# The up-projection's operands prepared one by one, and eight parked tiles set between full ones

## The chip, the cores and the metric

The kernel runs on one core of a Trainium2 chip. The metric is the device time of one execution in microseconds; lower is better. TensorE multiplies, VectorE and ScalarE do elementwise work, GpSimd helps with some of it, and SyncE's queue issues nearly all DMA transfers.

## The reference

Two layers of a diffusion backbone over 1024 latent tokens and 256 context tokens, width 1024. Each layer has a token-mixing part (attention, a linear recurrence, a Fourier mix) and a gated ConvFFN. The change concerns the FFN of the latent tokens:

```python
def conv_ffn(h, w_up, conv_w, conv_b, w_down):
    u = h @ w_up
    up = jnp.pad(u, ((0, 0), (1, 1), (0, 0)))
    u = up[:, :-2] * conv_w[0] + up[:, 1:-1] * conv_w[1] + up[:, 2:] * conv_w[2] + conv_b
    a, g = jnp.split(u, 2, axis=-1)
    return (a * jax.nn.silu(g)) @ w_down
...
        ffn = conv_ffn(x1 * (1 + sc2) + sh2, w_up[l], conv_w[l], conv_b[l], w_down[l])
```

`h` is 1024 x 1024, `w_up` 1024 x 5632 (2816 value columns, then 2816 gate columns), all in float32.

## The kernel before

**Products.** Each float32 operand is split into a rounded hi part (a cast on ScalarE) and a lo part (source minus hi, a subtraction). A product is the sum of three matmuls, lo x hi, hi x lo and hi x hi (`mm3`, lines 159 to 161).

**Tiles.** The up-projection has 22 tiles `j`. A tile is 128 value columns and the 128 gate columns that belong to them, over all 1024 tokens. It is computed by a 2 x 2 scheme with seven products instead of eight. The weights are the quarters A11, A12 (value columns, first and second half of the contraction) and A21, A22 (gate columns); S1 to S4 are sums of them. The stream `h` is cut into B11 and B21 (later half of the tokens, first and second half of the contraction) and B12, B22 (earlier half); T1 to T4 are differences of them. Each of these operands has four quarters of 128 contraction rows by 512 tokens, so a product is 4 x 3 = 12 matmuls of 512 columns and a tile 84. `ORDER` lists the seven pairs of a tile.

**Accumulation.** In `up_all` some products add onto the bank of an earlier one: S2 onto A11, S3 onto S2, S4 onto S1. Between them the bank is read: the result goes to U, two buffers of 1026 columns (value and gate), each with one column of padding at either end. A product with `onto` can only start when that read has been done. Seven PSUM banks serve the loop. When a tile is complete, `gate` runs the width-3 convolution (`conv`: one pass on ScalarE, two on VectorE), a SiLU on the gate part, and the product, and stores it to the scratch tensor `act`.

**Parked tiles.** For the first `EARLY` = 6 tiles the products A11 B11 and A12 B21 are computed ahead by `up_early`, because B11 and B21 are ready first: two tiles during the output projection's end, the others while `combined_halves` prepares T1 to T4 and B22. The first product and the sum of both are stored to the scratch tensor `parked`. In the loop these tiles come first, j = 0 to 5. Each has five products; the first parked product is loaded into the later half of `U[0]`, read by the additions behind S2 and S3, and then overwritten there by a load of the second:

```python
                if j < EARLY:
                    nc.sync.dma_start(out=U[0][:, late], in_=parked[j, 0])
```

**Preparation.** `combined_halves` goes quarter by quarter: it loads the four raw quarters of one k, scales and shifts them, forms T1 to T4 of that k and splits all five. GpSimd makes the lo parts of T1 and T4, VectorE the others.

**Weights.** `up_weights` loads 512 KB for the value part and for the gate part of each tile, forms S1 to S4 on VectorE and splits 512 columns at a time; `up_all` keeps five split weights ahead of the product in hand.

**Order.** The kernel is written as one listing per layer; a framework puts the instructions in an order on each engine by priorities and its own estimate of when operands are ready, so an engine's order can differ from the listing. During layer 0's loop the conditioning projection for layer 1 (`bg`, tiles `pada` and `araw`) takes single steps between products.

## Time and profile before

| | us |
|---|---|
| median of 3 runs | 3336.25 |
| lowest and highest of them | 3333.35, 3342.41 |
| the profiled execution, its own time | 3349.57 |
| its span | 3347.8 |
| TensorE busy in it | 3098.0 (93%) |
| VectorE busy | 2363.9 (71%) |
| ScalarE busy | 1585.6 (47%) |
| GpSimd busy | 772.6 (23%) |

A busy time is the sum of an engine's instructions in the profiled execution, as a share of the span from the first instruction to the last. Matmuls overlap in it, so TensorE's busy share doesn't say how many matmuls it could have taken in addition; counting matmuls in a window does. A wait is the idle time of an engine ahead of an instruction, put down to the work whose end released it. Tile names in a row are the program's: `pu` is a product's bank, `whi` and `wlo` the parts of a weight, `T2h` and `T2l` those of T2, `hraw` a raw quarter, `hcomb` a difference, `cv` a convolution's result, `up` the scratch tensor of parked products.

### The profile page before, as it was taken

The numbers are of one execution on the slowest core, as the hardware profiler recorded it, in microseconds if no ns is written. First come the engines' busy times: TensorE is split into PE (matmuls) and PEld (weight loads), VectorE is DVE, ScalarE is ACT, GpSimd is POOL, SyncE is SP. The second block draws the span as 40 slices with busy tenths as digits, with TensorE's granted clock in tenths as the row PEclk, the third lists the DMA queues.
The fourth block names the chain that finished last, engine by engine and source line by source line (L and its number), as shares of the span: only waits on it lengthen the run. The fifth ranks groups of instructions, "written<-read, shape, count | busy, mean of one in ns | idle before, by whom it ended". The sixth has DMA issues, their size and how long they took to land.

```text
span 3347.8 us, 55191 instructions
## 1 busy us (share of the span) xinstructions
PE 3098.0 (93%) x20897; PEld 2526.6 (75%) x20897; DVE 2363.9 (71%) x4377; ACT 1585.6 (47%) x3169; POOL 772.6 (23%) x820
## 2 busy tenths in 40 slices
PE   6999998999979999999999999998978789999996
PEld 4878977787756777677797788876767677887785
DVE  4623567887687877668876754668777778887678
ACT  3324556674444544434454435655652434554332
POOL 3522114432210000021245351115425300000222
PEclk9999999999989999999999999998889899999998
DMA  7652232107655444597775432122028632223973
GB/s 216 201 159 80 59 98 58 39 15 237 212 186 158 129 130 131 162 252 197 235 211 173 133 106 71 47 85 73 21 82 228 207 110 85 85 76 116 277 185 126
DMA packets 450255, 456.51 MB, mean 136 GB/s; under 512 B 31859, under 2 KB 343620, under 8 KB 449990
## 3 DMA queue, kind: packets, MB, share of 16 engines
q1 hardware_dynamic: 420006, 404.53, 38.4%
q0 software_dynamic: 29984, 48.46, 7.7%
q8 instruction: 164, 2.69, 0.3%
q14 instruction: 101, 0.83, 0.1%
HBM read 358.36 MB, written 94.55 MB: 135 GB/s over the span
## 4 chain that ended last, share of the span: by engine, by line
PE 47%; DVE 11%; DMA 5%; POOL 3%; issue 2%; ACT 2%; SPq 1%; POOLq 0%; DVEq 0%; ACTq 0%
PE pu L159 9%; PE pu L160 8%; PE pu L161 8%; PE pd L159 3%; PE pd L160 3%; PE pd L161 3%; PE ps_t L603 2%; PE ps_s L567 1%; PE ps_o L613 1%; DMA araw<-act 1%; DVE cv L1120 1%; DVE wlo L1387 1%; PE ps_s L568 1%; PE pws L159 1%; PE ps_o L615 1%
## 5 line engine op out<-in xcount | busy, mean ns | idle before, releaser
L570 DVE TENSOR_REDUCE mx<-ps_s 128x1 f32<-128x512 f32 (+1 forms) x400 | 222.4, 588 | 109.7 <-PE ps_s L568 108.6
L1345 POOL DMA_DIRECT2D X<-in_w_down_dram x48 | 55.4, 1154 | 1028.9 <-DMA X<-in_w_down_dram 945.1
L609 DVE TENSOR_TENSOR pl<-ps_t,ph 128x512 fp32r<-128x512 f32 x328 | 223.0, 686 | 88.1 <-ACT ph L608 86.1
L603 PE MATMUL ps_t<-ident,p 128*128 128x128 f32 x1312 | 265.5, 286 | 14.2 <-DVE pl L609 8.7
L608 ACT CAST ph<-ps_t 128x512 fp32r<-128x512 f32 x328 | 191.0, 589 | 162.8 <-PE ps_o L615 81.7
L577 ACT ACTIVATE p<-ps_s,mx 128x512 f32<-128x512 f32 (+1 forms) x400 | 243.2, 617 | 52.2 <-DVE mx L573 42.4
L160 PE MATMUL pd<-wlo,whi 128*128 128x512 f32 x616 | 248.4, 403 | 14.0 <-DVE wlo L1387 12.3
L159 PE MATMUL pd<-whi,wlo 128*128 128x512 f32 x616 | 242.8, 401 | 16.9 <-DVE wlo L1387 12.7
L1120 DVE SCALAR_TENSOR_TENSOR cv<-U,cw,cv 128x512 f32<-128x512 f32 x352 | 247.1, 748 | 12.9 <-ACT cv L1117 12.8
L161 PE MATMUL pd<-whi 128*128 128x512 f32 x616 | 247.7, 402 | 0.0
L159 PE MATMUL pxs<-whi,hlo 128*128 128x256 f32 x752 | 221.5, 295 | 5.8 <-DVE hraw L1566 4.3
L145 POOL TENSOR_TENSOR wlo<-raw,whi 128x1024 fp32r<-128x1024 f32 x63 | 152.5, 2423 | 281.0 <-ACT whi L144 281.0
L160 PE MATMUL pxs<-wlo,hhi 128*128 128x256 f32 x752 | 216.5, 288 | 0.6 <-DVE wlo L145 0.4
L161 PE MATMUL pxs<-whi,hhi 128*128 128x256 f32 x752 | 216.2, 288 | 0.0
L613 PE MATMUL ps_o<-pl,V 128*128 128x256 f32 x656 | 202.8, 326 | 6.6 <-DVE pl L609 4.0
L603 PEld LDWEIGHTS ps_t<-ident,p 128*128 128x128 f32 x1312 | 166.2, 144 | 38.2 <-DVE pl L609 14.7
L1117 ACT ACTIVATE cv<-U,cb,cw 128x512 f32<-128x512 f32 x176 | 138.1, 815 | 111.4 <-DVE U L1248 99.3
L615 PE MATMUL ps_o<-ph,V 128*128 128x256 f32 x656 | 184.7, 299 | 0.0
L1232 ACT CAST whi<-S 128x512 fp32r<-128x512 f32 x176 | 106.4, 620 | 149.2 <-PE pu L161 113.3
L144 ACT CAST whi<-raw 128x1024 fp32r<-128x1024 f32 x130 | 136.0, 1049 | 84.3 <-DMA raw<-in_w_up_dram 30.7
L567 PE MATMUL ps_s<-KT,qt 128*128 128x512 f32 (+1 forms) x400 | 150.8, 408 | 6.4 <-ACT p L577 3.0
L159 PEld LDWEIGHTS pxs<-whi,hlo 128*128 128x128 f32 x752 | 143.5, 191 | 15.3 <-issue 7.4
(401 smaller groups left out, 9160.4 us busy)
## 6 DMA issues: line engine op xcount, KB each, us to landing
raw<-in_w_up_dram SPq DMA_DIRECT2D x144, 512.0 KB
raw<-in_w_ada_dram SPq DMA_DIRECT2D x96, 512.0 KB
raw<-in_w_down_dram SPq DMA_DIRECT2D x52, 512.0 KB
act<-cv SPq DMA_DIRECT2D x88, 256.0 KB
X<-in_w_down_dram POOLq DMA_DIRECT2D x40, 512.0 KB, 9.6
raw<-in_w_in_dram SPq DMA_DIRECT2D x36, 512.0 KB
y<-r SPq DMA_DIRECT2D x28, 512.0 KB
araw<-act SPq DMA_DIRECT2D x26, 512.0 KB
```

The lines of the kernel that those rows point to most:

```text
L159: nc.tensor.matmul(o, lhsT=al, rhs=bh, start=start, stop=False, skip_group_check=onto)
L160: nc.tensor.matmul(o, lhsT=ah, rhs=bl, start=False, stop=False, skip_group_check=onto)
L161: nc.tensor.matmul(o, lhsT=ah, rhs=bh, start=False, stop=stop, skip_group_check=onto)
L567: nc.tensor.matmul(t[:, 0:n], lhsT=qt[:, h % (2 * QT_PAIRS), :], rhs=KT[:, 2 * kv + 1, s0:s0 + n], start=True, stop=False)
L570: nc.vector.tensor_reduce(out=mx[:, j:j + 1], in_=t[:, 0:n], axis=AX.X, op=ALU.max)
L577: nc.scalar.activation(out=t, in_=sc[j][:, 0:n], func=AF.Exp, bias=mx[:, 3:4], accum_out=su[:, h, j:j + 1])
L603: nc.tensor.transpose(t[:, ss, h, :], in_=ps2[h][2 * s2 + ss], identity=ident)
L608: nc.scalar.copy(ph, tv)
L609: nc.vector.tensor_tensor(out=pl, in0=tv, in1=f32(ph), op=ALU.subtract)
L613: nc.tensor.matmul(o, lhsT=V[:, s, kv, 1:3, :].rearrange("p a c -> p (a c)"), rhs=pl[:, ss, :], start=(s == 0), stop=False)
L615: nc.tensor.matmul(o, lhsT=V[:, s, kv, 0:2, :].rearrange("p a c -> p (a c)"), rhs=ph[:, ss, :], start=False, stop=(s == nk - 1))
L1120: nc.vector.scalar_tensor_tensor(out=o, in0=u[:, tap:tap + n], scalar=convw[l][tap][:, c:c + 1], in1=o, op0=ALU.mult, op1=ALU.add)
```

## The change

- `EARLY` goes from 6 to 8. The loop's order is `TURNS`: tile 8, then 9, 0, 10, 1, ... 16, 7, then 17 to 21, so that each parked tile stands between full ones.
- The first parked product is loaded into a ring `old` of two tiles of its own, and the additions read it there.
- `combined_halves` loads all sixteen raw quarters first, most into memory of operands that are written later, and finishes one operand after the other: T2, T1, T3, B22, T4. All lo parts are made on VectorE. Between the parked tiles two steps of it run instead of three.
- Six weights of the loop are split before the preparation ends (`ready_w`).
- `ORDER` has S4 B22 ahead of A22 T4.
- A weight split covers 1024 columns (A11 with A12, S2 with S1, S3 with S4), A22 512. The convolution covers 1024 columns, the value part first, and a tile is stored to `act` in one transfer.

```diff
--- before.py
+++ after.py
@@ -37,7 +37,7 @@
 GRID_W = 64
 ROPE_THETA = 10000.0
 NLEV = 7
-EARLY = 6
+EARLY = 8
 HELD = (2, 3)
 W_DVE = (0, 1)
 N_W = 2
@@ -1145,11 +1145,14 @@
     NK = NJ // 2
 
     def h_pair(hp, nm):
-        return tuple(hp.tile([P, 4, HALF], F32R, name=nm + x) for x in "hl")
+        return tuple([t[:, k, :] for k in range(4)] for t in (hp.tile([P, 4, HALF], F32R, name=nm + x) for x in "hl"))
 
     def load_quarter(rp, yT, t0, k, cols, tag, bufs, eng=None):
         r = rp.tile([P, HALF], F32, tag=tag, bufs=bufs, name="hraw")
         nc.sync.dma_start(out=r, in_=yT[k * P:(k + 1) * P, CTX + t0:CTX + t0 + HALF])
+        return modulated(r, k, cols, eng)
+
+    def modulated(r, k, cols, eng=None):
         a, b = (c[:, k:k + 1] for c in cols)
         if eng is nc.scalar:
             nc.scalar.activation(out=r, in_=r, func=AF.Identity, scale=a, bias=b)
@@ -1158,7 +1161,7 @@
         return r
 
     def split_to(pair, k, src, eng):
-        hi, lo = (t[:, k, :] for t in pair)
+        hi, lo = (t[k] for t in pair)
         nc.scalar.copy(hi, src)
         eng.tensor_tensor(out=lo, in0=src, in1=f32(hi), op=ALU.subtract)
 
@@ -1168,24 +1171,60 @@
             split_to(h["B11" if k < 4 else "B21"], k % 4, r, nc.gpsimd)
             yield
 
-    def combined_halves(h, rp, yT, cols):
+    def combined_halves(h, hp, rp, yT, cols):
+
+        def place(nm, k, dt=F32):
+            return (rp if nm[0:3] == "raw" else hp).tile([P, HALF], dt, tag=f"{nm}{k}", bufs=1, name=nm)
+
+        def fetch(nm, r, k, eng=None):
+            kk, t0 = k + 4 * (nm[1] == "2"), HALF if nm[2] == "1" else 0
+            nc.sync.dma_start(out=r, in_=yT[kk * P:(kk + 1) * P, CTX + t0:CTX + t0 + HALF])
+            return modulated(r, kk, cols, eng)
+
+        def sub(o, x, y):
+            nc.vector.tensor_tensor(out=o, in0=x, in1=y, op=ALU.subtract)
+            return o
+
+        def split_into(nm, k, src):
+            hi, lo = (place(nm + x, k, F32R) for x in "hl")
+            nc.scalar.copy(hi, src)
+            nc.vector.tensor_tensor(out=lo, in0=src, in1=f32(hi), op=ALU.subtract)
+            for t, x in zip(h[nm], (hi, lo)):
+                t.append(x)
+
+        for nm in ("T2", "T1", "T3", "T4", "B22"):
+            h[nm] = ([], [])
+        b11, b21, b12, b22, t1, t2 = ([] for _ in range(6))
         for k in range(4):
-            b11, b21, b12, b22 = (load_quarter(rp, yT, t0, kk, cols, f"raw{t0}{kk // 4}", 1 if t0 else 2, e)
-                                  for t0, kk, e in ((HALF, k, nc.scalar), (HALF, k + 4, nc.scalar), (0, k, None), (0, k + 4, None)))
+            b11.append(fetch("B11", place("T3h", k), k, nc.scalar))
+            b21.append(fetch("B21", place("B22l", k), k, nc.scalar))
             yield
-            t1, t2, t3, t4 = (rp.tile([P, HALF], F32, tag=f"t{x}", bufs=1, name="hcomb") for x in range(4))
-            for o, x, y in ((t1, b12, b11), (t2, b22, t1), (t3, b22, b12), (t4, t2, b21)):
-                nc.vector.tensor_tensor(out=o, in0=x, in1=y, op=ALU.subtract)
+        for k in range(4):
+            b12.append(fetch("B12", place("B22h", k), k, nc.scalar))
+            b22.append(fetch("B22", place("raw2", k), k))
+            t1.append(sub(place("T3l", k), b12[k], b11[k]))
+            t2.append(sub(place("raw1", k), b22[k], t1[k]))
+            split_into("T2", k, t2[k])
             yield
-            for nm, src, eng in (("T2", t2, nc.vector), ("T1", t1, nc.gpsimd), ("T3", t3, nc.vector), ("T4", t4, nc.gpsimd),
-                                 ("B22", b22, nc.vector)):
-                split_to(h[nm], k, src, eng)
+        for k in range(4):
+            split_into("T1", k, t1[k])
+            yield
+        for k in range(4):
+            split_into("T3", k, sub(place("T4h", k), b22[k], b12[k]))
+            yield
+
+        t4 = [sub(t2[k], t2[k], b21[k]) for k in range(4)]
+        for k in range(4):
+            split_into("B22", k, b22[k])
+            yield
+        for k in range(4):
+            split_into("T4", k, t4[k])
             yield
 
     def up_product(w, b, bank, onto=None):
         acc = psu([P, HALF], "pu", bank) if onto is None else onto
         for k in range(4):
-            mm3(acc, tuple(t[:, k, :] for t in w), tuple(t[:, k, :] for t in b), k == 0 and onto is None, k == 3,
+            mm3(acc, tuple(t[:, k, :] for t in w), tuple(t[k] for t in b), k == 0 and onto is None, k == 3,
                 onto is not None)
         return acc
 
@@ -1199,7 +1238,10 @@
         for x, t in enumerate((p1, c11)):
             nc.sync.dma_start(out=parked[j, x], in_=t)
 
-    ORDER = (("A11", "B11"), ("A12", "B21"), ("S2", "T2"), ("S1", "T1"), ("S3", "T3"), ("A22", "T4"), ("S4", "B22"))
+    ORDER = (("A11", "B11"), ("A12", "B21"), ("S2", "T2"), ("S1", "T1"), ("S3", "T3"), ("S4", "B22"), ("A22", "T4"))
+
+
+    TURNS = [EARLY] + [x for j in range(EARLY) for x in (EARLY + 1 + j, j)] + list(range(2 * EARLY + 1, NJ))
 
     def up_weights(l, fp):
         made = {}
@@ -1216,57 +1258,75 @@
             if (j, nm) not in made:
                 for o, x, y, op in (("S1", "A21", "A22", ALU.add), ("S2", "S1", "A11", ALU.subtract),
                                     ("S3", "A11", "A21", ALU.subtract), ("S4", "A12", "S2", ALU.subtract)):
-                    t = fp.tile([P, 4, P], F32, tag=o, bufs=1, name=o)
+
+                    pair = "S21" if o in ("S1", "S2") else "S34"
+                    if (j, pair) not in made:
+                        made[j, pair] = fp.tile([P, KD, P], F32, tag=pair, bufs=1, name="S")
+                    h = 4 * pair[1:].index(o[1])
+                    t = made[j, pair][:, h:h + 4, :]
                     nc.vector.tensor_tensor(out=t, in0=operand(j, x), in1=operand(j, y), op=op)
                     made[j, o] = t
             return made[j, nm]
 
         def splits(todo):
-            for n, (j, nm) in enumerate(todo):
-                if n % 2 == 0:
-                    own = n // 2 % 5 > 2
-                    pair = [(fp if own else wp).tile([P, 1024], F32R, tag=t + "x" * own, bufs=2 if own else 3, name=t)
-                            for t in ("whi", "wlo")]
-                hi, lo = (t[:, n % 2 * 512:n % 2 * 512 + 512].rearrange("p (a b) -> p a b", a=4) for t in pair)
-                src = operand(j, nm)
+            wide = 0
+            while todo:
+                j, nm = todo.pop(0)
+                if nm == "A22":
+                    hl, n = [fp.tile([P, 512], F32R, tag=t + "y", bufs=1, name=t) for t in ("whi", "wlo")], 4
+                    src = operand(j, nm)
+                else:
+                    todo.pop(0)
+                    own = wide % 4 == 3
+                    wide += 1
+                    hl = [(fp if own else wp).tile([P, 1024], F32R, tag=t + "x" * own, bufs=1 if own else 3, name=t)
+                          for t in ("whi", "wlo")]
+                    n = KD
+                    operand(j, "S4" if nm == "S3" else nm)
+                    operand(j, nm)
+                    src = made[j, {"A": 0, "S2": "S21", "S3": "S34"}[nm[0] if nm[0] == "A" else nm]]
+                hi, lo = (t.rearrange("p (a b) -> p a b", a=n) for t in hl)
                 nc.scalar.copy(hi, src)
                 nc.vector.tensor_tensor(out=lo, in0=src, in1=f32(hi), op=ALU.subtract)
-                yield hi, lo
-
-        todo = [(j,) + o for j in range(NJ) for o in ORDER if j >= EARLY or o[1] not in ("B11", "B21")]
+                for k in range(0, n, 4):
+                    yield hi[:, k:k + 4, :], lo[:, k:k + 4, :]
+
+
+        todo = [(j,) + o for j in TURNS for o in ORDER if j >= EARLY or o[1] not in ("B11", "B21")]
         return todo, splits([t[0:2] for t in todo])
 
-    def up_all(l, fp, todo, ws, h, parked, act, bg):
+    def up_all(l, fp, todo, ws, h, parked, act, bg, ahead):
         U = [fp.tile([P, SEQ + 2], F32, name=f"U{part}") for part in range(2)]
         for u in U:
             nc.vector.tensor_copy(u[:, 0:1], zcol[:, 0:1])
             nc.vector.tensor_copy(u[:, SEQ + 1:SEQ + 2], zcol[:, 0:1])
         late, early = slice(1 + HALF, 1 + SEQ), slice(1, 1 + HALF)
-        ahead = []
 
         def add(o, x, y, op=ALU.add):
             nc.vector.tensor_tensor(out=o, in0=x, in1=y, op=op)
 
         def gate(j):
+            cv = []
+            for part in (0, 1):
+                o = fp.tile([P, SEQ], F32, tag=f"cv{part}", bufs=1, name=f"cv{part}")
+                conv(l, j, part, o, U[part])
+                if part:
+                    nc.scalar.activation(out=o, in_=o, func=AF.Silu)
+                cv.append(o)
             for t0 in (HALF, 0):
-                cv = []
-                for part in (1, 0):
-                    o = fp.tile([P, HALF], F32, tag=f"cv{part}", bufs=2, name=f"cv{part}")
-                    conv(l, j, part, o, U[part][:, t0:t0 + HALF + 2])
-                    if part:
-                        nc.scalar.activation(out=o, in_=o, func=AF.Silu)
-                    cv.append(o)
+                v, g = (o[:, t0:t0 + HALF] for o in cv)
                 if (j < NK) == (t0 > 0):
-                    nc.vector.scalar_tensor_tensor(out=cv[1], in0=cv[1], scalar=-1.0, in1=cv[0], op0=ALU.mult, op1=ALU.mult)
+                    nc.vector.scalar_tensor_tensor(out=v, in0=v, scalar=-1.0, in1=g, op0=ALU.mult, op1=ALU.mult)
                 else:
-                    nc.vector.tensor_tensor(out=cv[1], in0=cv[1], in1=cv[0], op=ALU.mult)
-                nc.sync.dma_start(out=act[j, :, t0:t0 + HALF], in_=cv[1])
+                    nc.vector.tensor_tensor(out=v, in0=v, in1=g, op=ALU.mult)
+            nc.sync.dma_start(out=act[j, :, :], in_=cv[0])
 
         for j, a, b in todo:
             if a == [o for o in ORDER if j >= EARLY or o[0][0:2] != "A1"][0][0]:
                 got = {}
                 if j < EARLY:
-                    nc.sync.dma_start(out=U[0][:, late], in_=parked[j, 0])
+                    old = fp.tile([P, HALF], F32, tag="old", bufs=2, name="old")
+                    nc.sync.dma_start(out=old, in_=parked[j, 0])
             while len(ahead) < 5:
                 ahead.append(next(ws, None))
 
@@ -1281,7 +1341,7 @@
             elif a in ("S2", "S3"):
                 o = u2 if a == "S2" else u3
                 if j < EARLY:
-                    add(o, t, p1)
+                    add(o, t, old)
                 else:
                     nc.scalar.copy(o, t)
                 if a == "S3":
@@ -1720,14 +1780,19 @@
                 pass
         hgs.close()
         hp = h2s.enter_context(pool(f"h2c{l}", side=side_b))
-        h2.update({nm: h_pair(hp, nm) for nm in ("T1", "T2", "T3", "T4", "B22")[::-1 if side_b == "right" else 1]})
         ups = ExitStack()
         todo, uw = up_weights(l, ups.enter_context(pool(f"upw{l}", side=side_a)))
         with pool(f"pro{l}", side=side_a) as ep:
-            prep = combined_halves(h2, ep, yT, m2[0])
+            prep = combined_halves(h2, hp, ep, yT, m2[0])
             for j in range(2, EARLY):
                 up_early(l, j, h2, ep, "early", parked)
-                for _ in range(3):
+                for _ in range(2):
+                    next(prep, None)
+
+            ready_w = []
+            for n in (4, 2):
+                ready_w += [next(uw) for _ in range(n)]
+                for _ in range(4):
                     next(prep, None)
             for _ in prep:
                 pass
@@ -1735,7 +1800,7 @@
         act_d = scratch(f"act{l}", [NJ, P, SEQ])
         with pool(f"up{l}", side=side_a) as fp:
             bg = ada_all(1, [(i, u) for i in range(3) for u in range(2)], fp, 2, "araw", "g") if l == 0 else iter(())
-            last_gate = up_all(l, fp, todo, uw, h2, parked, act_d, bg)
+            last_gate = up_all(l, fp, todo, uw, h2, parked, act_d, bg, ready_w)
             for _ in bg:
                 pass
             f1, f2, f3 = [], [], []
```

## Rows read from the trace of the kernel before

**Rows 1.** Windows of layer 1's up-projection: stretch, length, each engine's busy time, clock, DMA.
```profile
2640.00:2820.00 180.00, 145.54 (x588) 114.29 (x587) 150.56 (x236) 78.03 (x126) 13.88 (x8) 0.91 0.37 113
2820.00:3080.00 260.00, 260.00 (x1123) 208.77 (x1122) 212.48 (x332) 132.33 (x215) 0.00 (x0) 1.00 0.26 80
```

**Rows 2.** Windows of layer 0: up-projection matmuls, then those of the conditioning.
```profile
920.00:1100.00 180.00, 143.55 (x564) 107.79 (x564) 26.18 (x38) 4.11 (x7) 0.92 0.54 169
1100.00:1380.00 280.00, 264.58 (x1091) 201.82 (x1090) 37.93 (x55) 23.52 (x40) 1.00 0.41 127
...
920.00:1100.00 180.00, 12.31 (x144) 3.28 (x144) 0.85 (x2) 0.92 0.54 169
1100.00:1380.00 280.00, 19.75 (x232) 4.83 (x232) 1.27 (x3) 1.00 0.41 127
```

**Rows 3.** TensorE's waits: layer 0's start, then layer 1's: total us, times, longest.
```profile
PE pu L159 <- ACT whi L1232: 19.5, 1, 19.5
...
PE pu L159 <- ACT whi L1232: 19.9, 1, 19.9
PE pu L159 <- DVE U L1248: 7.4, 4, 3.0
PE pu L159 <- DVE wlo L1233: 6.8, 3, 3.1
```

**Rows 4.** TensorE's timeline at layer 0's hole: start, length, engine, line, operation.
```profile
926.40 0.40 PE L161 MATMUL pu<-B21h,whi 128*128 128x512 f32 x1
946.29 0.77 PE L159 MATMUL pu<-T2h,wlo 128*128 128x512 f32 x1 [19.49 <-ACT whi L1232]
946.85 0.63 PE L160 MATMUL pu<-T2l,whi 128*128 128x512 f32 x1
```

**Rows 5.** VectorE's timeline in layer 0.
```profile
914.33 1.22 DVE L145 TENSOR_TENSOR wlo<-raw,whi 128x1024 fp32r<-128x1024 f32 x1
915.47 1.00 DVE L1157 TENSOR_SCALAR hraw<-hraw,ma,mb 128x512 f32<-128x512 f32 x2
916.38 1.29 DVE L1178 TENSOR_TENSOR hcomb<-hraw 128x512 f32<-128x512 f32 x2
...
921.19 2.36 DVE L1157 TENSOR_SCALAR hraw<-hraw,ma,mb 128x512 f32<-128x512 f32 x2
...
939.47 1.75 DVE L1163 TENSOR_TENSOR B22l<-hraw,B22h 128x512 fp32r<-128x512 f32 x1
...
965.13 3.39 DVE L1120 SCALAR_TENSOR_TENSOR cv<-U,cw,cv 128x512 f32<-128x512 f32 x5
968.44 0.69 DVE L1260 SCALAR_TENSOR_TENSOR cv<-cv,cv 128x512 f32<-128x512 f32 x1
```

**Rows 6.** GpSimd's timeline in the same stretch.
```profile
921.79 1.47 POOL L1163 TENSOR_TENSOR T4l<-hcomb,T4h 128x512 fp32r<-128x512 f32 x1
...
939.08 1.60 POOL L1163 TENSOR_TENSOR T1l<-hcomb,T1h 128x512 fp32r<-128x512 f32 x1 [1.61 <-ACT T1h L1162]
```

**Rows 7.** Timeline of one parked tile in layer 1, all engines.
```profile
2747.22 0.39 SPq L1269 DMA_DIRECT2D U<-up  x1
...
2751.92 0.69 DVE L1248 TENSOR_TENSOR U<-pu,U 128x512 f32<-128x512 f32 x1 [2.19 <-DMA U<-up]
...
2752.67 0.50 PE L159 MATMUL pu<-T3h,wlo 128*128 128x512 f32 x1 [3.01 <-DVE U L1248]
...
2757.30 0.69 DVE L1248 TENSOR_TENSOR U<-pu,U 128x512 f32<-128x512 f32 x1 [4.69 <-PE pu L161]
...
2759.54 0.39 PE L159 MATMUL pu<-B22h,wlo 128*128 128x512 f32 x1
...
2762.46 0.69 DVE L1248 TENSOR_TENSOR U<-pu,U 128x512 f32<-128x512 f32 x1
...
2769.05 0.32 SPq L1269 DMA_DIRECT2D U<-up  x1
```

**Rows 8.** Window ahead of layer 0's hole, all engines.
```profile
900.00:920.00 20.00, 20.00 (x91) 16.24 (x90) 10.91 (x17) 9.68 (x15) 2.20 (x1) 1.00 0.94 303
```

## The prediction

> **What bounds the kernel now.** I started with the windows, because a share over the whole span mixes stages. In layer 1 the stretch 2820 to 3080 us is the up-projection running steadily: 1123 matmuls in 260 us, TensorE busy throughout at a granted clock of 1.00 [rows 1]. That is 0.2315 us for a matmul, and TensorE is the bound there. The same table puts 588 matmuls into the 180 us before it, where VectorE is busy 150.6 us. At the steady rate they need 136.1 us, so 43.9 us are lost at the start of the stage.
>
> Layer 0 has conditioning matmuls for the next layer mixed in, so I split its windows by tile. From 1100 to 1380 us, 1091 up-projection matmuls take 252.6 us at the same rate, which leaves 27.4 us for 232 conditioning matmuls, 0.118 each. From 920 to 1100 us, 564 and 144 of them should take 130.6 + 17.0 = 147.6 us; 32.4 of the 180 us are lost [rows 2]. Together 76.3 us, and this is all that a change which leaves the number of matmuls as it is can win inside the stage.
>
> The waits of TensorE say where it goes [rows 3]. In each layer there is one hole, 19.5 and 19.9 us, between the last parked product and the first product with T2. The rest, 12.9 and 24.0 us, is a set of short waits on VectorE's additions to U and on weight splits, and matmuls at the lower clock after them: behind the hole matmuls take 0.77 and 0.63 us, before it 0.40 [rows 4]. Half the rate is TensorE's level of 1.2 GHz against 2.4 GHz.
>
> **Part 1, the hole.** Today every product of tile 0 needs an operand of which the fourth quarter comes last, so TensorE waits for the whole preparation. The change gives it work of its own in that time: two more tiles are parked (48 matmuls, 11.1 us), and the first tile in the loop is a full one, whose first two products need only B11 and B21 (24 matmuls, 5.6 us). After 926.6 us [rows 4] TensorE can go on to 937.7, then 943.3 us, before it needs T2. It needs T1 2.8 us later, T3 at 948.9, B22 at 951.7, T4 at 954.4.
>
> Can VectorE deliver? Its prices are the distances between back-to-back starts: 0.60 us for 512 columns, 1.14 us for a wide split, 0.45 us for a scaling pass (the second of two, 1.00 - 0.55) [rows 5]. From 914.3 us it has 4 scalings (1.8), 16 subtractions and 20 splits (21.6), about four of the six parked tiles (a wide split and an addition, 4 x 1.74 = 7.0), and tile 8's weights (4 sums, 3 wide splits, one narrow, 6.4): 36.8 us, so it ends at 951.1 us with T4, in the order of need. The sum closes 3 us ahead of TensorE. It has chains in it (each hi part is cast on ScalarE first; U takes the memory of the parked tiles and raw quarters, so its first copy waits for the split of the first B22 quarter). I keep 5 us of hole a layer; bounds are 0 and 12.
>
> That 21.6 includes 8 subtractions taken from GpSimd, 4.8 us more for VectorE. They are paid back: while GpSimd's subtractions run, VectorE instructions of the same kinds are stretched, 2.36 us for the pair that takes 1.00 elsewhere, and 1.75 us for a subtraction, of which two together take 1.29 [rows 5, 6]; six such places add 6.2 us in this stretch. My sum has none of them, since GpSimd gets nothing in the new code. The Trainium skill, "SBUF — State Buffer", section "Who interferes with whom", says the same as a mechanism: VectorE with two SBUF inputs and a reading GpSimd share a port, and the later one is blocked. By that rule the move costs 4.8 - 6.2 = -1.4 us; if the stretched rows had another cause, VectorE would end up to 6 us later.
>
> **Part 2, the parked tiles.** Follow one of them round in layer 1 [rows 7]. The reload of its first product into U starts only when the previous gate has read U (2747.22), VectorE's addition waits for it until 2751.92, product S3 accumulates onto the same bank and so starts at 2752.67, its addition comes at 2757.30, S4 follows at 2759.54, its addition at 2762.46, and when the convolutions have read U, the next reload at 2769.05: 21.8 us, while TensorE has 60 x 0.2315 = 13.9 us of work in such a tile. The run is bound by this ring, not by an engine.
>
> The change takes the reload out of it: the product goes to a ring of two tiles, which waits for no gate (-4.7 us). The convolution of U's first half follows S4 directly and is ScalarE's pass and two wide VectorE passes: with 1.20 us for a wide pass (the convolution's spacing of 0.66 us [rows 5] plus the 0.54 by which a wide split exceeds a narrow one), and 1.2 us on ScalarE as an estimate of the same size, 0.6 + 1.2 + 2.4 = 4.2 us instead of 6.6. S3 at full clock saves about 1.7. The ring is then near 13.1 us.
>
> The neighbours change too: a parked tile now alternates with a full one. TensorE needs 144 x 0.2315 = 33.3 us for the pair. VectorE needs, for the full tile, 4 sums, 3 wide splits and a narrow one, 4 additions, 4 wide convolution passes and 2 gate products, 2.4 + 4.0 + 2.4 + 4.8 + 1.2 = 14.8 us, and for the parked one 2.4 + 2.9 + 3.0 + 4.8 + 1.2 = 14.3: 29.1 us. By this TensorE bounds the pair. Before, six parked tiles in a row asked VectorE for 14.9 us each (narrow passes) against 13.9. I keep 3 us of loss in layer 0, where conditioning fills gaps, and 5 in layer 1; bounds are 0 and today's 12.9 and 24.0.
>
> **Part 3, what costs nothing.** Wide splits and convolutions save VectorE under 0.1 us an instruction; in the steady stretch it idles 47 of 260 us, so nothing is won. Two more tiles a layer are stored, reloaded, and have their value weights loaded twice: 4 stores, 4 reloads and 2 loads, on SyncE's queue. DMA is at 0.94 between 900 and 920 us [rows 8], but at 0.54 from 920 to 1100 [rows 2]: the cover is that slack. Without it the 2 MB of loads and stores cost 7 us a layer at 303 GB/s. The smaller rings of split weights are covered by the five products prepared ahead.
>
> **The sum.** 76.3 - 2 x 5 - 3 - 5 = 58 us. The profiled execution took 3349.57 us (span 3347.8), 13.3 above the median of the runs, so it would come to 3291.3, and the median from 3336.25 to 3278 us. A difference under 0.3% (10 us) can hardly be told from none.
>
> **Rivals.**
> A. Slower: S4 now stands directly behind S3, and A22, which lay between, behind both. S4 accumulates onto S1's bank, which must be read first: from the addition at 2757.30 to S4 at 2759.54 is 2.2 us [rows 7]. If TensorE's queue holds S4 with nothing before it, 44 tiles lose 97 us: 3336 - 58 + 97 = 3375. It decides above 58 / 44 = 1.3 us a tile. Against it: the queue is not in the listing's order today, and the steady stretch has no idle TensorE although S3 and S4 are coupled the same way. The Trainium skill, "TensorE: Matmul & The Clock Gate", section "Part 2: What happens when you issue a matmul", says that matmuls stay in program order, only weight loads being pulled ahead; so a badly placed S4 would hold all behind it, as A has it. Chance 0.07.
> B. The hole stays half: transfers or VectorE late by the 7 us above, in both layers. Gain 44, time 3292. For it: the DMA row at 0.94. Chance 0.20.
> C. The hole closes, but parked tiles stay bound by the ring, since VectorE works in a fixed order and its additions stand behind splits. Then 28.9 us less: 3307. Chance 0.15.
> D. Everything is recovered: 3260. Chance 0.10.
> Forecast: 0.48, own range 3266 to 3290. The range 3258 to 3312 takes in B, C and D and leaves out A and C's worst end. Slower: A, 0.06 of it. Same: the rest of A and a twentieth where B and C fall together, 0.06. Faster: 0.88.
>
> **What would show it.** In the new trace T2's first matmul starts within 8 us of the matmul before it; no GpSimd subtraction runs there; the stretch to the first steady tile has under 12 us of TensorE waits a layer; no addition to U waits on a reload; the number of up-projection matmuls is unchanged. I am wrong if TensorE's waits on VectorE's additions appear once a tile, or if a wait on weight or quarter loads takes the hole's place.

## The result and the profile after

The changed kernel takes 3304.70 us (median of 4 runs, 3302.41 to 3307.56), and beside it on the same chip the kernel before 3339.33 (4 runs): ratio 0.9895, interval 0.9877 to 0.9912, a gain of 35 us (29 to 41). Forecast were 58. The profiled span is 3303.3 us. The profiled execution of before lay some 10 us above its own median, so two profiles differ by 44.5 us, and differences between them are read against that.

First the windows of the two stages: in layer 1 all engines, in layer 0 the up-projection's matmuls and then the conditioning's [rows 1, 2].

```profile
2618.00:2798.00 180.00, 170.91 (x721) 137.25 (x720) 153.53 (x203) 83.68 (x104) 0.00 (x0) 0.96 0.40 126
2798.00:3040.00 242.00, 233.18 (x995) 183.74 (x994) 197.17 (x235) 104.05 (x114) 0.00 (x0) 1.00 0.29 92
...
925.00:1105.00 180.00, 160.67 (x653) 121.95 (x653) 24.82 (x36) 10.56 (x18) 0.98 0.55 171
1105.00:1380.00 275.00, 255.71 (x1050) 193.97 (x1050) 41.75 (x61) 15.90 (x27) 1.00 0.45 143
...
925.00:1105.00 180.00, 12.06 (x128) 2.91 (x128) 0.85 (x2) 0.98 0.55 171
1105.00:1380.00 275.00, 22.29 (x256) 5.43 (x256) 1.68 (x4) 1.00 0.45 143
```

With the prediction's prices (0.2315 us for an up-projection matmul, 0.118 for one of the conditioning) the first 180 us of layer 1 lose 180 - 721 x 0.2315 = 13.1 us and the next 242 lose 11.7. In layer 0 the first 180 us lose 180 - 151.2 - 15.1 = 13.7 and the next 275 lose 275 - 243.1 - 30.2 = 1.7. Together 40.2 of the 76.3 are still lost; by these windows 36 are won. So the start of each stage was mended by much. A loss of 11.7 us stands in layer 1 in a window that, before, 1123 matmuls filled without a pause; most of the parked tiles now run there, where before all of them ran in the first 180 us.

TensorE's waits, in layer 0's start, layer 1's start and layer 1's parked run, name both [rows 3]:

```profile
PE pu L159 <- DVE wlo L145: 7.6, 1, 7.6
...
PE pu L160 <- DVE T4l L1191: 2.3, 1, 2.3
...
PE pu L159 <- DVE wlo L145: 6.6, 1, 6.6
PE pu L160 <- DVE T4l L1191: 2.5, 1, 2.5
...
PE pu L159 <- DVE U L1306: 5.9, 5, 1.4
PE pu L159 <- DVE wlo L1290: 2.8, 3, 1.0
PE pu L159 <- ACT U L1346: 1.4, 2, 0.7
```

The hole of 19.5 us became one of 7.6 that ends with the weight split of the last parked tile, and one of 2.3 that ends with T4's. The first stands ahead of parked work and not behind it: from the stage's first B11 product at 896.71 to the hole TensorE ran the 14 products of seven parked tiles, and the eighth begins at 944.80. On TensorE's timeline in layer 0 [rows 4] it looks like this:

```profile
936.78 0.39 PE L161 MATMUL pu<-B21h,whi 128*128 128x512 f32 x1
944.80 0.77 PE L159 MATMUL pu<-B11h,wlo 128*128 128x512 f32 x1 [7.63 <-DVE wlo L145]
945.37 0.63 PE L160 MATMUL pu<-B11l,whi 128*128 128x512 f32 x1
```

VectorE's timeline in the same stretch [rows 5] shows what was late: the first modulation (scale and shift) of a quarter. From there to the last split of T4, 34.6 us, VectorE is busy 31.9; its longest pause, 1.92 us, waits for ScalarE's cast of a weight.

```profile
930.53 0.55 DVE L1160 TENSOR_SCALAR raw<-raw,ma,mb 128x512 f32<-128x512 f32 x1 [2.84 <-DMA raw<-yT]
...
943.43 1.22 DVE L145 TENSOR_TENSOR wlo<-raw,whi 128x1024 fp32r<-128x1024 f32 x1
...
960.31 2.49 DVE L1191 TENSOR_TENSOR B22l<-raw,B22h 128x512 fp32r<-128x512 f32 x4
962.71 2.49 DVE L1191 TENSOR_TENSOR T4l<-raw,T4h 128x512 fp32r<-128x512 f32 x4
```

And the queue that issues transfers: quarter loads (L1181) stand between the stores of parked products (L1239). A store waits for its product, and the loads behind it with it.

```profile
914.50 0.44 SPq L1181 DMA_DIRECT2D T3h<-yT  x1
...
934.07 0.32 SPq L1239 DMA_DIRECT2D up<-early  x1
934.43 0.44 SPq L1181 DMA_DIRECT2D raw<-yT  x1
934.92 0.45 SPq L136 DMA_DIRECT2D raw<-in_w_up_dram  x1
```

The queue's waits from 890 to 965 us put a number on it, in the store's wait for ScalarE's copy of a product:

```profile
SPq L1239 <- ACT early L1236: 16.7, 6, 5.2
```

Last, the ring of parked tiles in layer 1 [rows 7]: a full tile's S4 addition (2833.30), then the next parked tile's S2, S3 and S1 additions and its S4; ahead of them the S3 addition of an earlier parked tile, and its S4.

```profile
2809.56 0.69 DVE L1306 TENSOR_TENSOR U<-pu,old 128x512 f32<-128x512 f32 x1 [1.59 <-PE pu L161]
...
2811.04 0.50 PE L159 MATMUL pu<-B22h,wlo 128*128 128x512 f32 x1 [1.28 <-DVE U L1306]
...
2833.30 0.69 DVE L1306 TENSOR_TENSOR U<-pu,U 128x512 f32<-128x512 f32 x1
...
2835.10 1.22 DVE L1290 TENSOR_TENSOR wlo<-S,whi 128x1024 fp32r<-128x1024 f32 x1
...
2836.23 1.28 DVE L1120 SCALAR_TENSOR_TENSOR cv<-U,cw,cv 128x1024 f32<-128x1024 f32 x1
...
2841.03 0.69 DVE L1306 TENSOR_TENSOR U<-pu,old 128x512 f32<-128x512 f32 x1
...
2844.63 0.39 PE L161 MATMUL pu<-T3h,whi 128*128 128x512 f32 x1
...
2845.38 0.69 DVE L1306 TENSOR_TENSOR U<-pu,old 128x512 f32<-128x512 f32 x1
...
2846.10 0.69 DVE L1306 TENSOR_TENSOR U<-pu,U 128x512 f32<-128x512 f32 x1
...
2846.84 0.50 PE L159 MATMUL pu<-B22h,wlo 128*128 128x512 f32 x1 [1.12 <-DVE U L1306]
```

Nothing waits for a reload any more. From the full tile's addition (2833.30) to the parked tile's first (2841.03) there are 7.7 us, since VectorE works through a split, three convolution passes, two weight sums and both gate products first; S3 follows at 2842.07 without a wait. TensorE waits one product later. S3's last matmul starts at 2844.63; then VectorE adds S3's result (2845.38) and reads S1's bank (2846.10), and only then can S4, which accumulates onto that bank, start at 2846.84. VectorE isn't behind in this: S3's addition starts 0.4 us after S3's last matmul, and at 2809.56 VectorE was idle ahead of it. TensorE has too little between S3 and S4. Of the five waits on U in layer 1, four are of this kind: 1.28 us at 2811.04, 1.12 at 2846.84, 1.28 at 2952.51, and 1.41 at 3042.61 in the last tile. In these four tiles 1, 3, 1 and 0 matmuls stand between S3 and S4 in TensorE's order; in the other 18 tiles of the layer 6 or more, and no S4 there waits for an addition. The three waits on splits follow 6.8 us behind the first three of them. The pair of tiles from 2811.04 to 2846.84 takes 35.8 us; in two pairs before, T2's products start at 2679.08, 2712.40 and 2745.70, 33.3 us apart.

### The profile page after: what moved, and what is told of

Same layout as the page of the kernel before. It is cut to its first block, busy times and chain, and to the rows that moved or that the text cites. A ratio compares the mean times of both kernels' runs of the same rounds, so it can differ in the third digit from the quotient of the medians.

```text
span 3303.3 us, 54421 instructions
## 1 busy us (share of the span) xinstructions
PE 3087.3 (93%) x20897; PEld 2518.2 (76%) x20897; DVE 2333.5 (71%) x4097; ACT 1538.2 (47%) x2917; POOL 736.8 (22%) x804
## 4 chain that ended last, share of the span: by engine, by line
PE 50%; DVE 12%; DMA 6%; POOL 3%; issue 3%; ACT 2%; SPq 1%; POOLq 0%; DVEq 0%; ACTq 0%
PE pu L159 9%; PE pu L160 8%; PE pu L161 8%; PE pd L159 3%; PE pd L161 3%; PE pd L160 3%; PE ps_t L603 2%; DMA araw<-act 1%; PE ps_s L567 1%; PE ps_o L613 1%; DVE cv L1120 1%; PE ps_s L568 1%; PE pws L159 1%; PE ps_o L615 1%; PE pws L160 1%
## 5 line engine op out<-in xcount | busy, mean ns | idle before, releaser
L603 PE MATMUL ps_t<-ident,p 128*128 128x128 f32 x1312 | 263.9, 285 | 13.1 <-DVE pl L609 7.5
L1120 DVE SCALAR_TENSOR_TENSOR cv<-U,cw,cv 128x1024 f32<-128x1024 f32 x176 | 223.2, 1281 | 27.5 <-ACT cv L1117 27.1
L603 PEld LDWEIGHTS ps_t<-ident,p 128*128 128x128 f32 x1312 | 165.9, 144 | 36.3 <-DVE pl L609 13.1
L1289 ACT CAST whi<-S 128x1024 fp32r<-128x1024 f32 x88 | 92.1, 1051 | 150.7 <-PE pu L161 122.2
L159 PEld LDWEIGHTS pd<-whi,wlo 128*128 128x128 f32 x616 | 116.9, 191 | 47.6 <-DVE wlo L1447 11.5
```

Of the source, the lines that this page charges most:

```text
L159: nc.tensor.matmul(o, lhsT=al, rhs=bh, start=start, stop=False, skip_group_check=onto)
L603: nc.tensor.transpose(t[:, ss, h, :], in_=ps2[h][2 * s2 + ss], identity=ident)
L1120: nc.vector.scalar_tensor_tensor(out=o, in0=u[:, tap:tap + n], scalar=convw[l][tap][:, c:c + 1], in1=o, op0=ALU.mult, op1=ALU.add)
```

## The experiments

Times are medians, each compared with runs of the kernel before on the same chip. "Stage" is, in the profile, from the first B11 product of the loop's preparation to the first matmul of the down-projection, "to 150th" from there to its 150th matmul, both layers added.

```
kernel                  time      ratio (interval)         stage L0  stage L1  to 150th
before                  3339.33   1                           508.5     473.6    1081.1
after                   3304.70   0.9895 (0.9877-0.9912)      494.3     456.3    1036.0
x12 loop alone          3300.08   0.9870 (0.9850-0.9891)      486.4     447.4    1033.2
x11 preparation, wide   3324.99   0.9955 (0.9937-0.9974)      505.2     471.2    1064.9
x1 six parked           3305.09   0.9891 (0.9875-0.9906)      497.5     458.8    1041.5
x2 reload into U        3308.52   0.9900 (0.9882-0.9919)      495.2     463.3    1043.4
x4 parked in a row      3310.98   0.9906 (0.9890-0.9921)      493.7     466.0    1048.3
x3 old product order    3302.01   0.9874 (0.9856-0.9892)      486.6     455.4    1032.8
x5 splits on GpSimd     3304.22   0.9904 (0.9887-0.9922)      497.0     459.0    1040.3
x6 stores elsewhere     3307.02   0.9911 (0.9896-0.9927)      495.3     458.3    1038.9
x7 U's own memory       3307.16   0.9914 (0.9896-0.9931)      498.8     463.3    1040.7
x8 x3 + x6 + x7         3303.93   0.9902 (0.9887-0.9918)      498.5     466.2    1042.8
x9 weights ahead        3301.85   0.9878 (0.9858-0.9898)      491.3     458.5    1034.2
x10 x3 + x9 + a pad     3304.22   0.9877 (0.9852-0.9902)      490.1     458.3    1039.6
```

No version is measurably faster than the changed kernel: intervals of all but x11's overlap with its own.

**x1, x2, x4: one part of the loop undone.** x1 parks six tiles again, everything else new.

```diff
-EARLY = 8
+EARLY = 6
```

> Six parked tiles instead of eight, all else as in the changed kernel. Theory (the hole is filled by parked work): TensorE loses 48 matmuls a layer, 11.1 us, that stood in the time of the preparation, so the hole grows by 8 to 11 us a layer and the time by 16 to 22 us, to 3321 to 3327. Rival (the queue): the extra weight loads and stores of the two tiles are what delays the quarter loads on SyncE's queue (its stores wait 16.7 us for ScalarE's copies there), so without them the quarters come as much earlier, and the time stays at 3305, within 5.

x2 takes the ring of its own away from the parked products.

```diff
-old = fp.tile([P, HALF], F32, tag="old", bufs=2, name="old")
-nc.sync.dma_start(out=old, in_=parked[j, 0])
+nc.sync.dma_start(out=U[0][:, late], in_=parked[j, 0])
...
-add(o, t, old)
+add(o, t, p1)
```

> The first parked product is loaded into U again, as before, with no ring of its own. Theory (the parked tiles were bound by the ring through the reload): each of the 8 parked tiles a layer waits again some 2 to 4 us for the load; in layer 1 the time rises by 8 to 24 us, in layer 0 by half of that. Rival (the full neighbour covers it): a pair leaves TensorE 33.3 us of work, the reload hides in it, and the time stays at 3305, within 5.

x4 runs the parked tiles one after the other, tile 8 still first.

```diff
-TURNS = [EARLY] + [x for j in range(EARLY) for x in (EARLY + 1 + j, j)] + list(range(2 * EARLY + 1, NJ))
+TURNS = [EARLY] + list(range(EARLY)) + list(range(EARLY + 1, NJ))
```

> Tile 8, then the eight parked tiles in a row, then the full ones. Theory (the ring and VectorE's 14.3 us against TensorE's 13.9 in a parked tile): with the reload out of the ring a parked tile alone takes 15 to 17 us, 1 to 3 more than TensorE's work, so 8 to 24 us in layer 1 and half of that in layer 0. Rival (the ring of two loads did it all, the alternation is idle): 3305, within 5.

x1 gave the time of the changed kernel, not the 16 to 22 us more that were expected. Its hole is 12.4 us in layer 0 (6.1 on T4's cast, 3.5 and 2.8 on splits of T4 and T1) and 13.0 against 9.1 in layer 1; the waits behind it in layer 1 are 6.2 us against 10.1, with fewer parked tiles. Layer 1's parked runs of x2 and of x4, waits on the addition to U:

```profile
PE pu L159 <- DVE U L1306: 10.4, 10, 1.6
```

```profile
PE pu L159 <- DVE U L1306: 13.4, 12, 2.7
```

Against 5.9 in five waits, the ring of its own saves 4.5 us of waits in layer 1 and the alternation 7.5; the stage there is 7.0 and 9.7 us longer. That is well below the 28.9 us at stake in the prediction's rival C: it seems that with one of the two undone the other covers most of it; x11 below, without both, waits 16.3 us. In the timed medians none of the three can be told from the changed kernel.

**x3: the old order of the last two products.**

```diff
-ORDER = (..., ("S3", "T3"), ("S4", "B22"), ("A22", "T4"))
+ORDER = (..., ("S3", "T3"), ("A22", "T4"), ("S4", "B22"))
```

The split of S3 and S4 stays wide; its second half is handed out after A22's.

> A22 T4 stands between S3 and S4 again. Theory (S4 directly behind S3 costs the short waits on VectorE's additions that the new trace shows in full tiles, 5.9 us in layer 1 and 1.5 in layer 0): they go, and the time falls by 4 to 8 us. Rival (S4 first is worth it, since the convolution of the value part starts 2.8 us sooner): waits on the first copy into U come up instead, 1 us or more a tile, and the time rises by 10 us or more.

Layer 0's stage is 7.7 us shorter, of which the start of the down-projection gives 5.3 back. In layer 1 the waits on U are those of the changed kernel to the tenth:

```profile
PE pu L159 <- DVE U L1310: 5.9, 5, 1.4
```

This doesn't clear the product order, because in layer 1 the edit never reached TensorE. Cut into stretches of matmuls on one operand, TensorE's order there has 199 of them in either trace, and all 199 are the same: the framework places the products by its own estimates, and A22 stands where it stood. In layer 0 the order did change (185 stretches against 197), and there the stage is as short as that of x12 below, 486.6 us against 486.4, although x3 has the new preparation and all wide instructions. So in layer 0 the order does cost time in the stage, and in layer 1 it wasn't tested.

**x6, x9: an earlier start of the preparation.** x6 sends the stores of parked products through GpSimd's queue, so that no quarter load stands behind one.

```diff
-nc.sync.dma_start(out=parked[j, x], in_=t)
+nc.gpsimd.dma_start(out=parked[j, x], in_=t)
```

> The stores of parked products are issued by GpSimd's queue instead of SyncE's. Theory (the hole left over, 7.6 and 6.6 us, comes from SyncE's queue: a parked store waits there for ScalarE's copy, which stands behind quarters not yet landed, and the next quarter and weight loads stand behind the store): the loads are issued some 8 us sooner, the wait on the last parked tile's weight split falls below 3 us in both layers, and the two stages shorten by 8 to 12 us together. Rival (DMA bandwidth or VectorE bounds the preparation): the loads are issued sooner and land as late, and the hole stays within 2 us.

SyncE's queue and VectorE's first modulation, in layer 0 of x6:

```profile
918.17 0.32 SPq L1181 DMA_DIRECT2D raw<-yT  x1
918.89 22.98 SPq L136 DMA_DIRECT2D raw<-in_w_up_dram  x5
...
919.51 0.55 DVE L1160 TENSOR_SCALAR raw<-raw,ma,mb 128x512 f32<-128x512 f32 x1 [1.69 <-DMA raw<-yT]
```

The last quarter load is issued at 918.17 instead of 934.43, and the first modulation comes 28.0 us behind the first B11 product (891.5) instead of 33.8. Yet T4's split ends 67.4 us behind it instead of 68.5, and the hole is 4.3 + 3.6 and 6.1 + 3.6 us instead of 7.6 + 2.3 and 6.6 + 2.5. The stretch from the first modulation to the last split of T4 grew from 34.6 to 39.3 us; 1.8 of that is VectorE work (33.7 us busy against 31.9), the rest pauses, mostly for ScalarE's casts. TensorE gains nothing measurable.

x9 loads and splits a parked tile's weights one step ahead.

```diff
+w = None
 for j in range(2, EARLY):
-    up_early(l, j, h2, ep, "early", parked)
+    up_early(l, j, h2, ep, "early", parked, w)
+    if j < EARLY - 1:
+        w = early_w(l, j + 1)
     for _ in range(2):
         next(prep, None)
```

> The weights of the next parked tile are loaded and split ahead of the preparation's two steps that stand between two parked tiles, all else as in the changed kernel. Theory (the hole left over is the last parked tile's weight load, issued behind all quarter loads at 934.9 us, and its split behind VectorE's queue): the wait on that split, 7.6 and 6.6 us, falls below 1.5 us in both layers, the matmuls after it run at full clock, and the stages shorten by 12 to 18 us together, a median of 3287 to 3294. Rival (VectorE or DMA is full in this time): the wait moves to T2 or T4 and the stages shorten by less than 4 us.

The wait on the split is 4.3 and 7.3 us, T4's 2.9 and 3.1: 17.6 over both layers against 19.0. As the rival had it, the stages shorten by less than 4 us together, 0.8: loading the weights earlier is not enough.

**x5: T1's and T4's lo parts on GpSimd again.**

```diff
-nc.vector.tensor_tensor(out=lo, in0=src, in1=f32(hi), op=ALU.subtract)
+(nc.gpsimd if nm in ("T1", "T4") else nc.vector).tensor_tensor(out=lo, in0=src, in1=f32(hi), op=ALU.subtract)
```

> The lo parts of T1 and T4 are made on GpSimd again, all else as in the changed kernel. Theory (GpSimd's subtractions stretch VectorE's): VectorE has 4.8 us less of its own and gets about 6 us of stretched instructions, so the hole and the time stay within 3 us, and stretched rows (1.7 us for a subtraction that takes 0.69) come back. Rival (moving them to VectorE was a loss, since VectorE is the bound of the hole): the hole shrinks by up to 4.8 us a layer and the time falls to 3295 to 3300.

VectorE's rows in layer 0, then GpSimd's:

```profile
930.38 2.36 DVE L1185 TENSOR_TENSOR T3l<-B22h,T3h 128x512 f32<-128x512 f32 x2
...
933.27 1.49 DVE L1160 TENSOR_SCALAR raw<-raw,ma,mb 128x512 f32<-128x512 f32 x1
934.68 1.75 DVE L1191 TENSOR_TENSOR T3l<-T4h,T3h 128x512 fp32r<-128x512 f32 x1
...
930.00 1.59 POOL L1191 TENSOR_TENSOR T1l<-T3l,T1h 128x512 fp32r<-128x512 f32 x1 [3.58 <-ACT T1h L1190]
932.87 3.00 POOL L1191 TENSOR_TENSOR T1l<-T3l,T1h 128x512 fp32r<-128x512 f32 x2 [1.28 <-ACT T1h L1190]
```

Beside GpSimd's subtractions the pair that takes 1.29 us in the changed kernel takes 2.36 again, a subtraction of 0.69 takes 1.75. The hole's first wait is 10.4 and 9.9 us instead of 7.6 and 6.6, each stage 2.7 longer; the total can't be told from the changed kernel's.

**x7, x8: U in memory of its own,** so that its first copy needs no preparation buffer to be free.

```diff
-def up_all(l, fp, todo, ws, h, parked, act, bg, ahead):
-    U = [fp.tile([P, SEQ + 2], F32, name=f"U{part}") for part in range(2)]
+def up_all(l, fp, todo, ws, h, parked, act, bg, ahead, U):
...
+U = [upw.tile([P, SEQ + 2], F32, name=f"U{part}") for part in range(2)]
```

> U gets memory of its own instead of that of the parked tiles and raw quarters. Theory (tile 8's product S2 waits because the first copy into U must wait for the split of B22's first quarter): T2 comes right behind the first two products of the loop, the waits on T4's lo part (2.3 and 2.5 us) go, and the stages shorten by 4 to 6 us together. Rival (VectorE delivers T4 that late anyway, and the wait turns up elsewhere): within 2 us.

The T4 wait is gone. The price is at the other end (layer 1), where TensorE now waits for the down-projection's weights; that they wait for U's new place is argued, not shown:

```profile
PE pd L159 <- ACT whi L1445: 14.7, 2, 13.5
```

x8 joins x3's, x6's and x7's edits.

> Three edits together: A22 before S4, parked stores on GpSimd's queue, U in memory of its own. Theory: they act on different waits and add up; from the changed kernel's two stages (494.2 and 456.2 us in the profile) 8.4 us for the order (measured), 8 to 12 for the stores and 4 to 6 for U: 20 to 26 us less, a median near 3282. Rival (the waits share one cause, VectorE's work in the preparation): no more than the order alone, 3297 to 3302.

It pays the same 14.3 us there, and the parts don't add up.

**x10:** x3's and x9's edits, and an unused tile in the preparation's memory that moves the buffers U would share.

```diff
+ep.tile([P, 2 * (SEQ + 2)], F32, name="pad")
```

> Weights ahead, A22 before S4, and U's memory kept clear of the parked tiles and raw quarters by an empty tile at the bottom of the preparation's pool, so that U stays where it is. Theory: 12 to 18 us for the weights, 8.4 for the order, 4 to 6 for U, without the 7.6 and 12.8 us that U's other place costs at the end of the stages: the stages come to 922 to 928 us together and the median to 3275 to 3283. Rival: one bound behind all of them, and no more than the order's 8 us.

Hole 6.1 + 2.9 us in layer 0; nothing more than x3 or x9 alone.

**x11, x12: the change in two halves.** x11 is the changed kernel with the old loop: six parked tiles, tiles in their number's order, x2's reload, x3's order. The new preparation and all wide instructions stay.

```diff
-EARLY = 8
+EARLY = 6
...
+TURNS = list(range(NJ))
```

> The new preparation and the wide splits and convolutions alone: six parked tiles first in a row, the reload into U, A22 before S4, as before the change. Theory (preparation and loop only pay together, since a first tile that needs T2 leaves nothing to do in the hole): the hole is 15 us or more again and the parked run is bound by its ring, so the stages are 970 us or more together (982 before, 950 with the whole change). Rival (VectorE's relief is the gain): 955 to 962.

x12 is the kernel before with the loop's part alone: eight parked, alternated, a ring of their own. Preparation, GpSimd, narrow instructions and product order are the old ones; the weight ring has the new kernel's size.

```diff
-EARLY = 6
+EARLY = 8
...
-own = n // 2 % 5 > 2
+own = n // 2 % 4 == 3
...
+TURNS = [EARLY] + [x for j in range(EARLY) for x in (EARLY + 1 + j, j)] + list(range(2 * EARLY + 1, NJ))
...
-add(o, t, p1)
+add(o, t, old)
...
-for _ in range(3):
+for _ in range(2):
```

> The old preparation, quarter by quarter with GpSimd's part, and narrow splits and convolutions, with the new loop: eight parked tiles, each between full ones, and their ring. Theory (the loop's order is what pays: a full tile first, parked tiles covered by full ones): most of the gain is here, the stages at 955 to 965 us together, and the hole under 12 us. Rival (without operands finished one by one the loop waits as long as before): 972 or more.

x12: the window of layer 1's parked run, then TensorE's waits in layer 0's start and in that run.

```profile
2794.00:3033.00 239.00, 235.65 (x1011) 186.94 (x1009) 206.28 (x323) 117.98 (x189) 0.00 (x0) 1.00 0.30 98
```

```profile
PE pu L159 <- DVE wlo L145: 9.5, 1, 9.5
...
PE pu L159 <- ACT U L1280: 3.4, 5, 0.7
```

x11: waits in layer 0's start, then in layer 1's first 230 us.

```profile
PE pu L160 <- DVE T4l L1191: 3.8, 1, 3.8
...
PE pu L159 <- ACT T2h L1190: 2.6, 2, 1.7
PE pu L159 <- DVE U L1310: 1.4, 1, 1.4
PE pu L159 <- DVE wlo L1290: 1.4, 1, 1.4
...
PE pu L159 <- DVE U L1310: 16.3, 11, 3.0
```

The loop alone has the whole gain: 43 us by its ratio against 35, intervals overlapping. It has the old preparation and GpSimd, and its hole is 9.5 us in layer 0, as short as 7.6 + 2.3. Its layer-1 run loses 239 - 1011 x 0.2315 = 5.0 us, the changed kernel's 11.7, and a pair of tiles takes 34.2 us (first T2 product at 2809.26, then 2843.50) against 35.8. In all 22 tiles of that layer x12 has seven or more matmuls between S3 and S4, and none of its waits is an S4 waiting for an addition. The new preparation alone also takes the hole down, to 9.2 us in layer 0 (the four rows), but leaves the parked tiles bound by their ring: 16.3 us on additions to U in layer 1, where the kernel before had 7.4 and 6.8 on splits [rows 3]. It gains 15 us by its ratio (9 to 21 of 3342). So either half takes layer 0's hole to 9 or 10 us, and the two together close it no further; only the loop mends the ring.

## Why the prediction was right, and where it was too high

Faster, and inside the range; the gain fell short of the forecast 58, and the time lies above the own range of 3266 to 3290. By the windows 22.2 us more are left than the sum allowed: 13.7 + 13.1 in the holes against 2 x 5, and 1.7 + 11.7 behind them against 3 + 5. 58 - 22.2 = 36. That this meets the measured 35 is in part luck, as the paragraph on stages and end shows.

**Part 1, the work for TensorE: missed by one parked tile.** That TensorE ran to 937.2, with 937.7 forecast, is chance: the stage starts 4.7 us later than before (896.7 against 892.0), and only 168 of the 192 parked matmuls had run. The eighth tile's 24, 5.6 us, stood behind the hole, because their weights weren't split. The load of these weights is issued at 934.92, behind the quarter loads, and the split comes at 943.43. The sum counted this work as there and didn't ask when its weights are.

**Part 1, VectorE's sum: right in its prices, wrong in its start. This is the step that failed.** Forecast were 36.8 us "from 914.3". From the first modulation at 930.53 to T4's end at 965.2 there are 34.7, with part of the parked tiles' work done before. But it started 16 us later, 11.5 when both are counted from the stage's start, because eight quarter loads now stand ahead of the first pair that VectorE combines, on a queue where they lie between stores that wait for TensorE's products: 16.7 us of such waits. The prediction named queues and didn't follow this one. T4 then comes 14.1 us later than forecast, 9.4 from the stage's start, and TensorE, which would have waited for nothing, waits 9.9 us in two places, plus the products at the lower clock behind the hole. x6 shows that the start isn't all: with the loads issued early VectorE ends 1.1 us sooner. What remains is the chain through ScalarE's casts and VectorE, which is busy 31.9 of 34.6 us here, and 22.2 of the 23 us from 914 on in x12. Which part of that work would have to go wasn't tried.

**Part 1, credit: wrong.** The sum gave the closed hole to parked work and to operand order together. Each alone gets as far as both (x12, x11).

**Part 1, GpSimd: right.** No GpSimd subtraction and no stretched VectorE row is left between the first modulation and T4's end, and x5 brings both back with 2.7 us a stage. The Trainium skill, "SBUF — State Buffer", section "Who interferes with whom", says that a VectorE instruction with two SBUF inputs contends with a reading GpSimd; x5's 2.36 and 1.75 us agree.

**U's first copy: right.** It came at 961.07, behind the first B22 split at 960.31. TensorE ran T1 and T4 ahead of T2 meanwhile, which is the T4 wait; x7 removes it and pays elsewhere.

**Part 2, the ring: right.** The reload is out of it, and no parked tile's S3 waits for an addition in the changed kernel, where before it waited up to 3.01 us [rows 7]. The term "0.6 + 1.2 + 2.4 = 4.2 us" from the full tile's S4 addition to the parked tile's first was mis-sized, 7.7, but TensorE waits for nothing there.

**What the 5 us for layer 1 left out: S4 close behind S3.** The sum kept 5 us there and 11.7 were lost. The waits in layer 1's parked run and last tile are 10.1 us: 5.1 of S4 in the four tiles, 2.8 on splits in the tiles behind three of them, the rest on other copies and additions to U. The S4 waits are the mechanism of rival A, which the prediction priced at once a tile; it came in four tiles of 22. The split waits are of another kind: there VectorE has a wide convolution pass and the wide split in a row (2815.36 and 2816.55), and TensorE waits 0.96 us for the split at 2817.82.

**Part 3, "nothing": wrong, and its cause is only in part shown.** x12, with narrow instructions, the old preparation and the old order, gives the pair 34.2 us. In layer 0 the changed kernel's stage is 7.9 us longer than x12's, and in x3, with the old order and all wide instructions, 7.7 of these are gone, 2.1 of them in the hole. In layer 1 TensorE's order differs between x12 and the changed kernel too, and x3 didn't change it there; order, wide instructions with their rings and preparation remain together. That the order is the larger part is argued from where the waits stand; no run sets it alone in layer 1. A smaller slip: the "2 MB" of Part 3 leaves out the two weight loads of 512 KB each; with them it is 3.1 MB, 10 us a layer at 303 GB/s.

**Stages and end.** The table's stages are 31.5 us shorter than before, the way to the 150th matmul of the down-projection 45.1. So 13.6 us come from that stretch, which no term of the sum has, while the stages give less than the windows' 36. For x12 it is 48.3 and 47.9: there a microsecond of the stage is one of the kernel. The stretch takes 99.0 us before, 99.4 in x12 and 85.4 in the changed kernel, both layers added. In all three its DMA share is 1.03 to 1.05; layer 1 of the changed kernel, of x12 and of before:

```profile
3046.00:3086.00 40.00, 35.64 (x147) 27.22 (x148) 24.36 (x25) 16.33 (x19) 10.04 (x9) 1.00 1.05 305
```

```profile
3033.00:3083.00 50.00, 37.26 (x147) 29.31 (x147) 25.29 (x29) 18.99 (x23) 9.07 (x8) 0.90 1.03 306
```

```profile
3085.00:3135.00 50.00, 37.97 (x150) 29.67 (x151) 26.96 (x31) 18.75 (x23) 10.03 (x9) 0.87 1.05 305
```

Of the three, before ends its stages last and x12 first, and both take equally long; so it isn't a matter of how soon the stage ends. What goes with it is how far the transfers have got by then. The last 10 us of layer 1's stage, changed kernel and x12:

```profile
3036.00:3046.00 10.00, 7.59 (x31) 5.27 (x29) 3.95 (x5) 4.62 (x6) 0.26 (x1) 1.00 0.77 247
```

```profile
3023.00:3033.00 10.00, 10.00 (x44) 7.84 (x42) 4.55 (x6) 4.70 (x6) 0.00 (x0) 1.00 0.51 172
```

In all the kernels of the table, layer by layer, the first 150 matmuls take 49 to 51 us where the DMA share of the 10 us ahead of them was 0.37 to 0.57, and 38 to 46 us where it was 0.62 or more. That the transfers set this stretch is argued from these rows; no run changed them. Last, the two profiles differ by 44.5 us and the medians by 35: some 10 us are the slower profiled execution of before, and the profiles don't say in which stage they lie.

Rival B (3292) comes near the truth in its hole. Rival C (3307) meets the time by its number; its mechanism, additions behind splits, isn't what the rows show. A's happened in a few tiles, D not at all. Of the signs of being wrong one came, the wait on a weight split in the hole's place. Of the signs of being right one failed in layer 1, where TensorE's waits up to the steady tiles are 9.1 + 8.0 us and not under 12.

## What to carry to other kernels

When a stage's start is bound by a preparation, ask first when that preparation can begin: follow its loads through the queue that issues them, and note each store ahead of them that waits for the very engine you are feeding. Ask the same of the filler: a parked tile fills a hole only when its own weights are ready. Two ways to fill one hole don't add up, so price the second with the first in place, and look at what the next stage waits for before you count a stage's gain as the kernel's. When a framework orders the instructions, a changed listing need not change the engine's order: compare the order in both traces before you call it tested.

## What the runs showed of the hardware

A scaling on VectorE, with one tensor as its input, is stretched beside GpSimd's subtractions as a subtraction is, 1.49 us against 0.54 (x5). After a pause of 7.6 us TensorE's matmuls take 0.77 and 0.63 us as after one of 19.5 [rows 4], and nearly as many of them, 9 against 11; the granted clock is 0.50 from 944 to 948 us in the changed kernel, the level of 1.2 GHz. In layer 1 eight of the matmuls behind a wait of 2.54 us do the same, 0.60 to 0.73 us each. So a short hole costs nearly the same behind it as a long one.
